# Splitting the first load of A on SyncE's queue into 32 and 96 partitions, in a batched 64x64 matmul

## The chip, the cores and the metric

The kernel runs on one core of a Trainium2 chip. The metric is the device time of one execution in microseconds (us); lower is better. Times come as a median of several runs; one further execution was recorded by the hardware profiler, and its trace is what the times of single instructions are read from.

## The reference

```python
def setup_inputs():
    return {
        "a": np.random.randn(1024, 64, 64).astype(np.float32),
        "b": np.random.randn(1024, 64, 64).astype(np.float32),
    }

def reference(a, b):
    return np.matmul(a, b).astype(np.float32)
```

There are 1024 independent products of two 64x64 matrices. A and B are 16.8 MB each and the output is as large, so 33.55 MB are read from HBM and 16.78 MB are written.

## The kernel before, in words

The 1024 products are cut in 16 steps `t` of 64 products for B and the output, and in 8 pairs of steps `s` of 128 products for A. One quarter `h` of a pair's A holds the matrices `4g + h`, with `g` from 0 to 31; each matrix is laid on four partitions, so a quarter is a tile of 128 partitions, each with one contiguous row of 1024 fp32 (4 KB). In HBM a quarter is 32 blocks of 16 KB, one block for each `g`.

A is converted to bf16, its 64x64 matrices are transposed in pairs of bf16 seen as one fp32, either on TensorE (`transpose`, L136, with copies out of PSUM by ScalarE at L144) or on VectorE (`transpose_dve`, L119; for the pairs 1, 2 and 3), and `spread` (L149) copies them into a block-diagonal weight tile `at_bd`. `cast` (L172) converts a step of B to bf16. `multiply` (L190) runs 64 matmuls a step against the block-diagonal weights and moves the results from PSUM to `o_sb`, mostly on ScalarE (L209). A step's output is stored one step later by `store`.

Loads go out on three DMA queues, in the order in which the program issues them:

- SyncE's queue (in the profile SPq, and q1 in the table of DMA queues): two quarters of the first A, B for the even steps, and the raw fp32 quarter `a_raw` of the later pairs of A.
- ScalarE's queue (ACTq, q10): the other two quarters of the first A, and B for the odd steps.
- GpSimd's queue (POOLq, q0): the converting loads of A to bf16 (`cast_load_a`, L70) and nearly all stores.

The order of the instructions is written out by hand under `tc.manual_schedule()`; tile pools and their semaphores decide only what waits. A load's completion is counted on a semaphore, and eight of these are shared in turn by the loads of SyncE's and ScalarE's queues; a load that takes a semaphore again waits for the load that had it.

The change is in `load_first_a` (L84). It borrows two output buffers `o_sb` for the four fp32 quarters `h` = 0 to 3 of pair 0, and issues quarters 0 and 2 on SyncE's queue and 1 and 3 on ScalarE's (L94). They are the first instructions on both queues. `regroup(0)` (L103) then converts the quarters into `a_bf` (L109), 0 and 2 on VectorE and 1 and 3 on ScalarE. On VectorE that comes after the clearing of `at_bd` (L250), and GpSimd clears the other block-diagonal tile in the same time (L252, L255). After the four conversions come 16 transposes of TensorE (L141), `spread(0)`, the cast of the first B on ScalarE, and the first `multiply`. The step loop (L262) runs the spread and the cast of step `t + 1` ahead of the multiply of `t`, and issues the B load of step `t + 3`.

Of the kernel before, what the change touches and what calls it, by code (L numbers as in the profile page):

```python
# [13 lines left out]
def kernel(  # L14
# [14 lines left out]
    nc = tc.nc  # L29
# [11 lines left out]
    a_v = a.rearrange("(s g h) (mp v) k -> s h g mp (v k)", h=4, g=32, v=16)  # L41
# [42 lines left out]
    def load_first_a():  # L84

        raw = [
            o_pool.tile([128, 8, 2, 2, 64], fp32, name="o_sb")[:].rearrange(
                "p gh j wl n -> p (gh j wl n)"
            )
            for _ in range(2)  # L90
        ]
        parts = [raw[h % 2][:, 1024 * (h // 2) : 1024 * (h // 2) + 1024] for h in range(4)]
        for h in range(4):
            (nc.scalar if h % 2 else nc.sync).dma_start(out=parts[h], in_=a_v[0, h])  # L94
        a_tiles[0] = parts

    def load_b(t):
# [144 lines left out]
    with tc.manual_schedule():  # L242
        first_cast = cast_load_a(1)
        load_first_a()

        nc.vector.memset(warm[:, 0:1], 0.0)
# [76 lines left out]
```

## Time and profile before

| | before |
|---|---|
| median of 3 runs | 133.37 us (133.36 to 133.55) |
| the profiled execution | 133.69 us |
| its span, first to last instruction | 131.8 us |
| VectorE (DVE) busy | 102.0 us, 77% |
| ScalarE (ACT) busy | 88.1 us, 67% |
| TensorE (PE) matmuls busy | 60.3 us, 46% |
| GpSimd (POOL) busy | 33.2 us, 25% |
| DMA queues q0, q1, q10, share of 16 engines | 52.7%, 28.5%, 20.2% |
| HBM traffic over the span | 382 GB/s |

The span is cut in 40 slices of 3.3 us in the page of the profile, and each digit of a row there is the busy share in tenths. A DMA share can be over 1, as the packets of one DMA engine overlap a little. In the tables of instructions, SPq and ACTq are the sequencers that issue DMAs; the time of such an issue is not the time of the transfer. A wait is put down to the instruction or the DMA that ended it. The profiled execution is 0.32 us longer than the median of the runs, and 1.89 us of its time lie outside its span.

### The profile page before, as it was taken

How to read it: one execution, taken by the hardware profiler on the slowest of the kernel's cores; microseconds unless marked ns; L12 is line 12 of the kernel's file. 1: busy time of each engine (PE TensorE's matmuls, PEld its weight loads, DVE VectorE, ACT ScalarE, POOL GpSimd, SP SyncE). 2: the span in 40 equal slices, each digit the busy share in tenths (PEclk: the TensorE clock that was granted, in tenths of full speed). 3: DMA queues.
4: the chain of work that ended last, by engine and by line, in shares of the span. 5: the costliest groups of instructions: out<-in, count | busy, mean ns of one | idle time of the engine just before them, and what ended most of it. 6: DMA issues, size and time to landing. Idle time of an engine off the chain costs nothing.

```text
span 131.8 us, 2749 instructions
## 1 busy us (share of the span) xinstructions
PE 60.3 (46%) x1104; PEld 57.2 (43%) x1104; DVE 102.0 (77%) x144; ACT 88.1 (67%) x158; POOL 33.2 (25%) x45
## 2 busy tenths in 40 slices
PE   0003701964090270908971983199369615366000
PEld 0003501964090270908961963198368614355000
DVE  5932099807999996999999999599999997798300
ACT  2123605599949069492999989559969998339930
POOL 6991000042016300618120204300420212041200
PEclk9999999999999998555599599559968999679755
DMA  3999999999999999999999999999999999999993
GB/s 71 344 341 306 306 306 297 270 313 319 328 316 401 347 310 308 399 390 395 314 288 364 400 397 359 306 303 389 393 390 392 395 391 393 391 405 402 402 379 135
DMA packets 18252, 44.99 MB, mean 341 GB/s; under 512 B 1088, under 2 KB 2112, under 8 KB 18240
## 3 DMA queue, kind: packets, MB, share of 16 engines
q0 software_dynamic: 7120, 21.24, 52.7%
q1 hardware_dynamic: 6064, 13.63, 28.5%
q10 hardware_dynamic: 5056, 9.96, 20.2%
q8 instruction: 8, 0.13, 0.4%
q14 instruction: 4, 0.03, 0.1%
HBM read 33.55 MB, written 16.78 MB: 382 GB/s over the span
## 4 chain that ended last, share of the span: by engine, by line
DMA 53%; ACT 16%; DVE 14%; PE 6%; issue 5%; SPq 2%; DVEq 0%; ACTq 0%
DMA b_sb<-in_b_dram 53%; ACT o_sb L209 13%; PE o_ps L221 5%; DVE at_bd L167 4%; DVE b_bf L176 4%; DVE at_bd L157 2%; ACT b_bf L176 1%; DVE at_sb L131 1%; DVE o_sb L209 1%; DVE a_bf L112 1%; SPq L94 1%; ACT a_bf L129 1%; SPq L100 1%; ACT b_bf L183 1%; DVE a_bf L115 0%
## 5 line engine op out<-in xcount | busy, mean ns | idle before, releaser
L209 ACT COPY o_sb<-o_ps 64x512 f32<-64x512 f32 x112 | 65.0, 581 | 18.5 <-PE o_ps L221 14.3
L221 PEld LDWEIGHTS <-at_bd 128*128 128x128 bf16 x1024 | 45.3, 117 | 51.5 <-DVE b_bf L176 39.6
L221 PE MATMUL o_ps<-b_bf,at_bd 128*128 128x64 bf16 x960 | 45.7, 223 | 47.1 <-DVE b_bf L176 36.8
L167 DVE COPY at_bd<-at_sb 32x1024 f32<-32x1024 f32 x40 | 29.5, 737 | 5.9 <-ACT at_sb L144 4.9
L198 POOL DMA_DIRECT2D out_dram<-o_sb x16 | 17.1, 1068 | 53.8 <-ACT at_sb L144 21.1
L157 DVE COPY at_bd<-at_sb 32x512 f32<-32x512 f32 x48 | 21.6, 451 | 1.1
L73 POOL DMA_DIRECT2D a_sb<-in_a_dram x21 | 12.0, 588 | 37.2 <-DVE at_sb L131 34.0
L176 DVE CAST b_bf<-b_sb 128x2048 bf16<-128x2048 f32 x14 | 17.4, 1245 | 4.3 <-DMA b_sb<-in_b_dram 4.0
L141 PE MATMUL at_ps<-identity,a_bf 128*128 128x128 f32 x80 | 13.3, 336 | 11.9 <-ACT a_bf L109 11.9
L141 PEld LDWEIGHTS at_ps<-identity,a_bf 128*128 128x128 f32 x80 | 12.2, 181 | 11.9 <-issue 11.9
L144 ACT COPY at_sb<-at_ps 128x512 f32<-128x512 f32 x20 | 10.8, 591 | 2.4 <-PE at_ps L141 2.0
L131 DVE STREAM_TRANSPOSE at_sb<-a_sb 128x512 f32<-128x512 f32 x9 | 8.7, 1055 | 0.0
L131 DVE STREAM_TRANSPOSE at_sb<-a_bf 128x512 f32<-128x512 f32 x3 | 3.1, 1044 | 4.6 <-ACT a_bf L129 4.6
L109 ACT CAST a_bf<-o_sb 128x1024 bf16<-128x1024 f32 x2 | 2.1, 1045 | 5.9 <-DMA o_sb<-in_a_dram 5.9
L209 DVE COPY o_sb<-o_ps 64x512 f32<-64x512 f32 x8 | 5.5, 689 | 0.2
L109 DVE CAST a_bf<-o_sb 128x1024 bf16<-128x1024 f32 x2 | 3.2, 1599 | 2.9 <-DMA o_sb<-in_a_dram 2.9
L176 ACT CAST b_bf<-b_sb 128x2048 bf16<-128x2048 f32 x1 | 1.9, 1899 | 4.5 <-DMA b_sb<-in_b_dram 4.5
L112 DVE COPY a_bf<-a_sb 128x3072 bf16<-128x3072 bf16 x4 | 4.2, 1046 | 0.0
L183 ACT CAST b_bf<-b_sb 128x512 bf16<-128x512 f32 x2 | 1.1, 614 | 4.5 <-DMA b_sb<-in_b_dram 4.5
L250 DVE MEMSET at_bd<- 128x4096 f32 x1 | 3.5, 3472 | 0.8 <-issue 0.8
L209 DVE COPY o_sb<-at_ps 64x256 f32<-64x256 f32 x8 | 3.4, 422 | 0.5 <-PE at_ps L221 0.4
L129 ACT CAST a_bf<-a_raw 128x1024 bf16<-128x1024 f32 x3 | 3.1, 1045 | 0.1
(16 smaller groups left out, 15.4 us busy)
## 6 DMA issues: line engine op xcount, KB each, us to landing
out_dram<-o_sb POOLq DMA_DIRECT2D x14, 1024.0 KB, 21.5
a_sb<-in_a_dram POOLq DMA_DIRECT2D x21, 256.0 KB, 14.2
a_raw<-in_a_dram SPq DMA_DIRECT2D x7, 512.0 KB, 17.5
o_sb<-in_a_dram SPq DMA_DIRECT2D x2, 512.0 KB, 6.8
o_sb<-in_a_dram ACTq DMA_DIRECT2D x2, 512.0 KB, 7.5
out_dram<-o_sb POOLq DMA_DIRECT2D x2, 512.0 KB, 5.9
out_dram<-o_sb SPq DMA_DIRECT2D x2, 256.0 KB, 4.6
out_dram<-o_sb ACTq DMA_DIRECT2D x2, 256.0 KB, 4.6
```

What stands on the lines that cost most here:

```text
L73: nc.gpsimd.dma_start(out=a_sb[:, h, :, :].rearrange("p v k -> p (v k)"), in_=a_v[s, h], single_packet=True)
L109: copy(a_bf[:, :, h, :], a_sb[h].rearrange("p (v k) -> p v k", v=16))
L112: nc.vector.tensor_copy(a_bf[:, :, 0:3, :], cast_sb[:].rearrange("p h v k -> p v h k"))
L131: nc.vector.transpose(at_tiles[s][:, h].rearrange("p g w mp vo -> p w vo g mp"), pairs.rearrange("p (vo w kp) -> p w vo kp", vo=4, w=4),)
L141: nc.tensor.transpose(at_ps[:, vo, :], a_cols[:, 4 * vo + 2 * j + wl, :], identity[:])
L144: nc.scalar.copy(at_tiles[s][:, :, 2 * j + wl, :, :], at_ps[:].rearrange("p vo (g mp) -> p g mp vo", mp=4),)
L157: nc.vector.tensor_copy(bd[rows, 8 * i : 8 * i + 8, :, h, :, :].rearrange("p g w mp vo -> p (g w) (mp vo)"), at_sb[block : block + 32, h]. ...
L167: nc.vector.tensor_copy(bd[rows, :, :, h, :, :].rearrange("p g w mp vo -> p (g w) (mp vo)"), at_sb[rows, half].rearrange("p g w mp vo -> p ...
L176: (nc.vector.tensor_copy if t else nc.scalar.copy)(b_bf[:], b_sb[:])
L198: store_queue(t, lo).dma_start(out=o_v[t, :, lo : lo + n, :], in_=o_sb[:, lo : lo + n].rearrange("p gh j wl n -> p (gh j wl n)"),)
L209: copies[2 * par + wl](dst, src)
L221: nc.tensor.matmul(o_ps[:, gl, g % 2, j, :], at_bd[:, j, g, :, u], b_bf[:, g, 64 * u : 64 * u + 64], start=(u == 0), stop=(u == 1),)
```

## The change

The load of quarter 0 is issued as two loads on the same queue: blocks `g` = 0 to 7, which are partitions 0 to 31, and then blocks `g` = 8 to 31, which are partitions 32 to 127. The bytes, the rows of 4 KB and the destination are the same. Quarters 1, 2 and 3 are loaded as before. VectorE's conversion of quarter 0 is not split, so it needs both parts. On SyncE there is one DMA instruction more; the instructions of the other engines and their order are unchanged. As one load more takes a semaphore, the later loads of SyncE's and ScalarE's queues each take the next one in turn.

```diff
         for h in range(4):
-            (nc.scalar if h % 2 else nc.sync).dma_start(out=parts[h], in_=a_v[0, h])
+            queue = nc.scalar if h % 2 else nc.sync
+            for lo, hi in ((0, 8), (8, 32)) if h == 0 else ((0, 32),):
+                queue.dma_start(out=parts[h][4 * lo : 4 * hi], in_=a_v[0, h, lo:hi])
         a_tiles[0] = parts
```

The lines of the kernel after this place are numbered two higher in the kernel after.

## The prediction

> **What bounds the kernel now.** I read the page's slices first, then the DMA queues, then the timeline of the first 24 us, then the DMA packets of its first stage, VectorE's waits and the chain that ended last.
>
> ```profile
> DVE  5932099807999996999999999599999997798300
> DMA  3999999999999999999999999999999999999993
> q0 software_dynamic: 7120, 21.24, 52.7%
> q1 hardware_dynamic: 6064, 13.63, 28.5%
> q10 hardware_dynamic: 5056, 9.96, 20.2%
> ```
>
> The DMA engines are full from the second slice to the last but one; the queues' shares add up to 101% of 16 engines. VectorE is nearly full from slice 10 to 35. So a transfer is late because of what is queued ahead of it, and more work on the DMA engines can't be made up by an earlier issue.
>
> ```profile
> 0.74 1.28 SPq L94 DMA_DIRECT2D o_sb<-in_a_dram  x2
> 1.69 3.47 DVE L250 MEMSET at_bd<- 128x4096 f32 x1 [0.83 <-issue]
> 2.49 0.73 SPq L100 DMA_DIRECT2D b_sb<-in_b_dram  x1
> 3.27 7.69 SPq L81 DMA_DIRECT2D a_raw<-in_a_dram  x1
> 5.17 2.50 DVE L109 CAST a_bf<-o_sb 128x1024 bf16<-128x1024 f32 x1
> 6.46 1.05 ACT L109 CAST a_bf<-o_sb 128x1024 bf16<-128x1024 f32 x1 [2.65 <-DMA o_sb<-in_a_dram]
> 10.58 0.69 DVE L109 CAST a_bf<-o_sb 128x1024 bf16<-128x1024 f32 x1 [2.90 <-DMA o_sb<-in_a_dram]
> 10.76 1.04 ACT L109 CAST a_bf<-o_sb 128x1024 bf16<-128x1024 f32 x1 [3.25 <-DMA o_sb<-in_a_dram]
> 11.42 0.71 SPq L100 DMA_DIRECT2D b_sb<-in_b_dram  x1
> 11.90 3.65 PE L141 MATMUL at_ps<-identity,a_bf 128*128 128x128 f32 x16 [11.90 <-ACT a_bf L109]
> 20.71 1.90 ACT L176 CAST b_bf<-b_sb 128x2048 bf16<-128x2048 f32 x1 [4.54 <-DMA b_sb<-in_b_dram]
> ```
>
> The columns are start, duration, instruction and, in brackets, the idle time before it and what ended it. The conversion of quarter 0 (5.17) has no DMA wait: it starts when the memset is done at 5.16. The trace has the quarter landing at 5.14. VectorE then sits idle for 2.90 us until quarter 2 is there. So quarter 0 itself is not on the path; quarters 2 and 3 (landing at 10.55 and 10.74) are, since TensorE's transposes wait for the last conversion. The first B load, third on SyncE's queue, is next: ScalarE waits 4.54 us for it.
>
> ```profile
> DVE b_bf L176 <- DMA b_sb<-in_b_dram: 4.0, 3, 1.6
> 102.61 14.88 DMA b_sb<-in_b_dram
> ```
>
> The first line is the only large wait of VectorE after 36 us; the second, from the chain in order of time, is the last B load, which brings ScalarE to the final step at 117.5. The path keeps coming back to a transfer, and it is the last of a transfer's 16 completions that counts: of the B load behind the wait of 1.6 us, fifteen came by 82.37 and the sixteenth at 83.71; of the last B load, fourteen by 116.07 and the others at 117.01 and 117.49. One or two DMA engines run behind the rest.
>
> **The issue.** One DMA issue more on SyncE. L94's two take 1.28 us together, 0.64 each with the pause between them; this bounds a 32-partition issue from above, the 0.38 us of the small final stores from below. Behind it on SyncE: the rest of quarter 0, quarter 2, the first B, the first `a_raw`. Each is issued 0.4 to 0.64 us later. For quarter 2 and B that is hidden, since their predecessors on the queue are still moving; for `a_raw` too, whose issue already stands 7.69 us because the queue is full. Counted at nothing. Without that cover it would be the whole 0.64.
>
> **The semaphores.** The counters move on by one, so the third B load (11.42), which had waited for none, now waits for the first part. That is there by about 5, and SyncE is held in the `a_raw` issue until 10.96: nothing. The `a_raw` loads after it wait for quarter 1 (landed 6.44) and for the second part instead of quarters 0 and 1, and ScalarE's first in-loop B load for quarter 3 instead of 2: all landed long before. Without SyncE's hold, the third B load alone would wait, for some 2 us.
>
> **The conversion.** It needs both parts. If the second lands 0.64 late, it starts at 5.8 instead of 5.17 and ends at 8.3, before quarter 2. The 2.90 us of idle time hide it; they cover a delay of up to 2.9 us.
>
> **The DMA engines.** This is the term that counts. A full quarter has 32 blocks in HBM and can be dealt evenly to 16 engines: 8 rows of 4 KB each. The parts have 8 and 24 blocks. The trace shows no load of this shape, so I bound it: dealt row by row the parts put 8 rows on each engine as before, at a cost of 0; dealt in whole blocks from the first engine on, 8 blocks reach 8 engines with 4 rows each, and 24 blocks divide evenly over 12 at most, 8 rows each. Then eight engines carry 12 rows, four carry 8 and four none. A row's price is in the first stage:
>
> ```profile
> DMA packets 338, 1.16 MB, mean 291 GB/s; under 512 B 31, under 2 KB 31, under 8 KB 338
> q1 hardware_dynamic: 149, 0.54, 48.9%
> q10 hardware_dynamic: 143, 0.52, 35.5%
> ```
>
> This is the window from 2 to 6 us, 64 engine-us. q10's 35.5% are 22.7 us; 0.52 MB are 127 rows; 0.18 us a row. q1's, with the cold start in it, are 0.24. I take 0.18, from the warmer queue, because the added rows come after the first. Four more rows are 0.72 us on eight engines (0.96 by q1's price). As these engines have no pause to give it back in, it stays in every later transfer that has its last completion there, up to the end. The upper bound is the queue order: with three queues in turn, each of the four rows lets one packet of each of the others pass. A row and a packet of each other queue at some 0.18 us, the small B packets at half, are 0.45 us, so four turns make 1.8 us for quarter 2 and the first B. Below nothing is possible too, by the four relieved engines, below. I take 0.72: the load on the path goes by total work, not by turns, once later queues are full; the turns' 1.8 is a high end for the start only, and VectorE's 4.0 us of waits can take some of it in.
>
> The Trainium skill ("DMA: Bandwidth & Descriptors", "Why a DMA increments its semaphore by 16 and not by 1") says that a DMA from SyncE uses the largest number of engines up to 16 that divides the outermost sizes of both its sides, the lowest-numbered ones: 8 and 12 here. By it the whole-block case is the one that happens, and the sum is the same 0.72; no run here shows it yet. The same page's "Rules for kernel authors" says that a transfer split into disjoint partition parts gains nothing, as the parts share the engines. By that rule alone the term would be 0, or the 0.64 of an issue.
>
> **The sum.** 0 + 0 + 0 + 0.72 us against the profiled 133.69 us: 134.41. The profiled execution stands 0.32 above the median, so I expect 134.1 as a median (133.37 + 0.72).
>
> **The rivals.** First, no change. The rows are dealt evenly, or the engines that bound the end are the four that keep 8 rows. For it: all loads of the trace make 16 completions, and the only load touched is off the path by 2.9 us. Against it: nothing in an 8-block load makes an even deal natural. Time: 133.4, within 0.2% (0.27 us), about what a measurement of this kernel can tell.
>
> Second, faster, by one mechanism: the DMA engines that run behind lie among the four relieved ones. These lose 8 rows, 1.44 us. The waits at 83.71 and 117.49 end with one and two late completions; if the late ones move up by 1.44, the next engine decides, 1.34 earlier in the first place (82.37) and 1.42 in the second (116.07) less the 0.72 that this one may have gained: 0.6 to 0.7 net. Time: 132.7. It decides only when both late engines of the second place are among the four; one alone leaves 117.01 or later. Against it: the last stores, whose completions form an early group of seven (129.20 to 129.92) and a late one of nine (130.31 to 130.77), so that at least one of the late nine is among the eight with more rows.
>
> Third, the turns of the queue count in full: quarter 2 lands at 12.3, the first B at 22.5, ScalarE's cast and all that follows it start 1.8 us later, and VectorE, 90% busy and more from there on, doesn't give it back. Time: 135.2. Against it: VectorE waits for B three times later on, and a full DMA queue does not care when it was filled.
>
> **How the numbers follow.** The forecast, 133.7 to 134.6, has 0.5; the third rival 0.11 (134.6 to 135.2); no change 0.16; faster 0.23. Slower by over 0.2% is then 0.61. The range has to leave out no more than 2 in 10: from 132.8, most of the faster case, to 135.1, most of the turns. The likeliest case's own range is 133.7 to 134.6.
>
> **What would show it.** Right: three issues of quarter loads on SyncE; the second part landing at 5.5 to 6; VectorE's first conversion starting with the DMA as its releaser; quarters 2 and 3 landing at 11.2 to 12 and the first transposes at 12.5 or later; the first B at 21.4 or later; the DMA slices as full as before, and the last stores 0.7 later. Wrong: quarter loads landing when they did (the even deal), or the start later and the end not (VectorE's waits took it in), or completions of the late B loads closing up (the relief). A start as forecast with an end that moved for another cause would refute the step in which the load is carried to the end.

## The result, and the profile after

The kernel after takes 135.82 us as a median of 4 runs (135.65 to 135.94), the one before 133.39: 2.43 us slower, a ratio of 1.0179 with a 95% interval of 1.0164 to 1.0195. The way was forecast, the size was not: 134.1 with a range up to 135.1. The profiled execution took 135.78 us, its span is 134.0. One run of all those below (141.74 us, the split 8 + 8 + 16 of the later quarters) was slow, 1.5% longer than the fastest of its kernel, and is left out.

The page's slices and queues of the kernel after, as they were shown of before:

```profile
DVE  5502208990899999899999999499999999598700
...
DMA  3999999999999999999999999999999999999994
...
q0 software_dynamic: 7120, 21.24, 52.1%
q1 hardware_dynamic: 6068, 13.63, 28.4%
q10 hardware_dynamic: 5056, 9.96, 21.0%
```

The bytes are the same and the DMA engines are as full (the three queues add up to 101.5% of 16 engines). VectorE stands at 0, 2, 2 and 0 tenths in slices 3 to 6, where it had 3, 2, 0 and 9: its first spreads come a slice later. The timeline of the start, kernel after (columns as in the prediction):

```profile
0.74 2.51 SPq L96 DMA_DIRECT2D o_sb<-in_a_dram  x3
...
4.52 11.17 SPq L81 DMA_DIRECT2D a_raw<-in_a_dram  x1
4.89 1.04 ACT L111 CAST a_bf<-o_sb 128x1024 bf16<-128x1024 f32 x1 [1.35 <-DMA o_sb<-in_a_dram]
...
10.96 1.04 ACT L111 CAST a_bf<-o_sb 128x1024 bf16<-128x1024 f32 x1 [5.02 <-DMA o_sb<-in_a_dram]
12.56 0.69 DVE L111 CAST a_bf<-o_sb 128x1024 bf16<-128x1024 f32 x1 [7.39 <-DMA o_sb<-in_a_dram]
15.52 0.69 DVE L111 CAST a_bf<-o_sb 128x1024 bf16<-128x1024 f32 x1 [2.27 <-DMA o_sb<-in_a_dram]
16.36 3.65 PE L143 MATMUL at_ps<-identity,a_bf 128*128 128x128 f32 x16 [16.36 <-DVE a_bf L111]
...
24.38 1.90 ACT L178 CAST b_bf<-b_sb 128x2048 bf16<-128x2048 f32 x1 [3.75 <-DMA b_sb<-in_b_dram]
```

VectorE now waits 7.39 us for the second part of quarter 0, which lands at 12.46 (the whole quarter landed at 5.14). That is not what holds the start up: the conversion that now comes last and releases TensorE's transposes is that of quarter 2, which lands at 15.50 instead of 10.55, behind the second part on its queue. The transposes start 4.5 us later, the first B lands 3.7 us later (24.36). ScalarE's and GpSimd's first loads gained: quarter 1 landed at 4.87 instead of 6.44. The first packet on SyncE's queue started at 3.85 us instead of 2.19, behind ScalarE's at 2.17.

The first part shows 8 completions of transfers (4.88 to 5.32), the second 12 (11.31 to 12.46); the rest of the sixteen is added at once at the start (2.09 and 2.92). This is the deal that the Trainium skill's rule gave ("DMA: Bandwidth & Descriptors", "Why a DMA increments its semaphore by 16 and not by 1"), and here trace and rule agree.

What the queues did from 8 to 12 us, first before, then after:

```profile
DMA packets 573, 1.29 MB, mean 322 GB/s; under 512 B 61, under 2 KB 61, under 8 KB 573
...
q0 software_dynamic: 192, 0.33, 44.2%
q1 hardware_dynamic: 189, 0.46, 32.2%
q10 hardware_dynamic: 192, 0.49, 31.1%
```

```profile
DMA packets 385, 0.96 MB, mean 241 GB/s; under 512 B 47, under 2 KB 47, under 8 KB 385
...
q1 hardware_dynamic: 127, 0.46, 44.6%
q0 software_dynamic: 129, 0.23, 31.0%
q10 hardware_dynamic: 129, 0.27, 30.8%
```

The engines are full in both, but a packet takes longer: on SyncE's queue 44.6% of 64 engine-us over 127 packets are 0.22 us, where it had been 0.11 (partly small B packets then); 4 KB rows alone took 0.18 to 0.32 us there instead of 0.17. ScalarE's packets went from 0.10 to 0.15 us, though fewer of them were large; GpSimd's stayed at 0.15, its 4-byte packets included.

To compare executions I count **work done**: every packet at what its kind usually takes in the kernel before (4 KB rows 0.171 us on SyncE's queue and 0.160 on ScalarE's, 2 KB packets 0.095 and 0.084 as in the first 20 us, 1 KB 0.047, GpSimd's loads 0.172 and stores 0.168), summed and divided by 16. It is an estimate, good to about 0.1 us. The kernel after is 0.1 us of such work behind before at 6 us, 1.4 at 12 us and still at 30 us, and 2.2 to 2.3 from 36 to 120 us; the two spans differ by 2.2 us. So two places lose the time: 6 to 12 us, and 30 to 36 us. In both it is lost by slower packets and not by idle DMA engines: counted as the packets really took, the DMA engines were busy for the same time up to 13.4 us within 0.1 us, and within 0.2 up to 50 us. The second place, from 30 to 34 us, before and after:

```profile
q1 hardware_dynamic: 169, 0.60, 40.9%
q0 software_dynamic: 166, 0.31, 40.9%
q10 hardware_dynamic: 170, 0.35, 23.6%
```

```profile
q1 hardware_dynamic: 253, 0.76, 60.0%
q10 hardware_dynamic: 270, 0.55, 44.8%
```

After, GpSimd's queue (q0) has nothing to move from 29.1 to 34.8 us; before, that pause lasted 0.4 us. Its next loads wait for a buffer that VectorE's transposes of pair 1 free, and these are late. The waits, before and after:

```profile
POOL a_sb L73 <- DVE at_sb L131: 34.0, 3, 15.6
```

```profile
POOL a_sb L73 <- DVE at_sb L133: 38.1, 3, 20.2
```

The longest of the three waits is 4.6 us longer. The other two queues fill the engines and move as many bytes (1.31 MB after, 1.28 before), but with slower packets: 4 KB rows at 0.19 to 0.21 us, B's 2 KB at up to 0.12. Why they are slower without GpSimd's beside them is not shown. ScalarE's queue is empty for a while too (20.9 to 29.4 us after, 20.2 to 27.1 before), and nothing is lost there.

### The profile page after: what moved, and what is told of

Same layout as the page of the kernel before. It is cut to its first block, busy times and chain, and to the rows that moved or that the text cites. A ratio compares the mean times of both kernels' runs of the same rounds, so it can differ in the third digit from the quotient of the medians.

```text
span 134.0 us, 2751 instructions
## 1 busy us (share of the span) xinstructions
PE 61.8 (46%) x1104; PEld 58.8 (44%) x1104; DVE 100.3 (75%) x144; ACT 88.1 (66%) x158; POOL 33.0 (25%) x45
## 3 DMA queue, kind: packets, MB, share of 16 engines
q1 hardware_dynamic: 6068, 13.63, 28.4%
## 4 chain that ended last, share of the span: by engine, by line
DMA 39%; DVE 23%; ACT 18%; PE 7%; issue 6%; SPq 2%; ACTq 1%; DVEq 0%
DMA b_sb<-in_b_dram 39%; ACT o_sb L211 15%; DVE at_bd L159 8%; PE o_ps L223 7%; DVE b_bf L178 5%; DVE at_bd L169 4%; DVE at_sb L133 4%; SPq L96 2%; ACT b_bf L178 1%; ACT a_bf L131 1%; DVE o_sb L211 1%; DVE a_bf L114 1%; ACTq L102 1%; ACT b_bf L185 1%; DVE a_bf L117 0%
## 5 line engine op out<-in xcount | busy, mean ns | idle before, releaser
L223 PEld LDWEIGHTS <-at_bd 128*128 128x128 bf16 x1024 | 46.5, 119 | 48.8 <-DVE b_bf L178 37.1
L223 PE MATMUL o_ps<-b_bf,at_bd 128*128 128x64 bf16 x960 | 47.0, 226 | 44.6 <-DVE b_bf L178 35.3
L169 DVE COPY at_bd<-at_sb 32x1024 f32<-32x1024 f32 x40 | 29.4, 735 | 5.4 <-ACT at_sb L146 4.4
L111 DVE CAST a_bf<-o_sb 128x1024 bf16<-128x1024 f32 x2 | 1.4, 694 | 9.7 <-DMA o_sb<-in_a_dram 9.7
```

The lines of the kernel that those rows point to most:

```text
L169: nc.vector.tensor_copy(bd[rows, :, :, h, :, :].rearrange("p g w mp vo -> p (g w) (mp vo)"), at_sb[rows, half].rearrange("p g w mp vo -> p ...
L223: nc.tensor.matmul(o_ps[:, gl, g % 2, j, :], at_bd[:, j, g, :, u], b_bf[:, g, 64 * u : 64 * u + 64], start=(u == 0), stop=(u == 1),)
```

## The experiments

Each kernel was timed in rounds against the kernel before on the same chip, except one that was executed once more, which is named. In the text, "later" and "slower" are against before. The table at the end of this section has the profiled executions in one view.

**Even parts.** 64 and 64 partitions instead of 32 and 96.

```diff
-            for lo, hi in ((0, 8), (8, 32)) if h == 0 else ((0, 32),):
+            for lo, hi in ((0, 16), (16, 32)) if h == 0 else ((0, 32),):
```

> Quarter 0 split as 64 + 64 partitions (16 + 16 blocks), still two loads on SyncE's queue. Theory U (uneven deal: 8 and 12 engines instead of 16 put 12 rows on eight engines and slow the rows): with 16 blocks each part is dealt to 16 engines, so the loss is gone: 133.2 to 133.8 us. Theory L (lost lead: one more issue on SyncE ahead of the bulk of quarter 0 lets ScalarE's and GpSimd's loads go first, and SyncE's later loads are served in turns behind them): the loss stays, 135 us or more, with quarter 2 landing after 14 us and the first B after 23 us.

134.66 us, 1.0068 [1.0046, 1.0090]. Between the two theories: 1.4 of the 2.4 us go with the uneven deal, 1.0 us stays. Sixteen completions for each part; quarter 2 lands at 12.66, the first B at 22.46.

**Even deal with the same sizes.** 32 and 96 partitions, but from consecutive rows in HBM (`a_rows`, a view of A by rows). The data are others, so the products of the first quarter are not those of the reference.

```diff
-                queue.dma_start(out=parts[h][4 * lo : 4 * hi], in_=a_v[0, h, lo:hi])
+                rows = a_v[0, h, lo:hi] if h else a_rows[0, 4 * lo : 4 * hi]
+                queue.dma_start(out=parts[h][4 * lo : 4 * hi], in_=rows)
```

> The split 32 + 96 of the kernel after, but quarter 0 is read from 128 consecutive rows of A instead of its own blocks (other data: the first quarter's products are of the wrong matrices). The HBM side's outermost size is then 32 and 96, both multiples of 16, so both parts are dealt to 16 engines, two and six rows each. Theory U: 133.2 to 133.8 us, sixteen completions for each part. Theory L: as the kernel after, 135.5 us or more, since the number of issues and their sizes are the same. If only the shift of the rows against the partitions slows them (96 rows over 16 engines do not sit as 128 do), rows of 0.25 us and more are seen here too.

134.02 us, 1.0024 [1.0013, 1.0036]. Sixteen completions for each part. So two loads of 32 and 96 partitions cost only 0.4 us here; the rest of the 2.4 goes with the blocks. That is more than the deal over engines: the rows lie side by side in HBM, the three issues took 1.54 us together instead of 2.51, and SyncE's first packet came at 1.76, ahead of ScalarE's (2.18), so this kernel does not separate slow rows from the lost lead. On SyncE's queue rows of 0.21 to 0.26 us are seen only from 5 to 6 us.

**The same split on quarter 2.**

```diff
-            for lo, hi in ((0, 8), (8, 32)) if h == 0 else ((0, 32),):
+            for lo, hi in ((0, 8), (8, 32)) if h == 2 else ((0, 32),):
```

> The same split in 8 and 24 blocks, but of quarter 2, the second load on SyncE's queue; quarter 0 is whole and leads. Theory U: the same uneven rows, in the same queue, so the same loss: 135.4 to 136 us. Theory L: SyncE's queue keeps its lead of 8 rows, so most of the loss is gone: 133.4 to 134.2 us, first B landing at 20.7 to 21.5 us.

135.32 us, 1.0120 [1.0099, 1.0141]. SyncE leads again (first packet 2.17, quarter 0 whole at 4.84), and two thirds of the loss stay. The lost lead seems the smaller part. Rows on both hardware queues are slow from 8.5 to 12 us, when the 96-partition part moves.

**A small load first.**

```diff
+        nc.sync.dma_start(out=small[:], in_=a_rows[0, 0:128, 0:16])
         for h in range(4):
```

> The kernel before, with one small load (128 rows of 64 bytes, into a tile that nothing reads) ahead of quarter 0 on SyncE's queue; all loads are dealt to 16 engines. Theory U: no uneven rows, so 133.3 to 133.8 us. Theory L: quarter 0 is issued one issue later (0.64 us), ScalarE's quarter 1 goes first, and the loss is as in the kernel after: 135 us or more.

(`small` is a tile that nothing reads.) 134.68 us, 1.0075 [1.0055, 1.0094], with no uneven deal at all: between the two theories. Its executions differ, from 133.72 to 135.09, and the profiled one was the fastest. It was executed and profiled once more, on another chip:

> The kernel with the small load ahead of quarter 0, profiled once more. If its usual 134.7 us comes from a late start of the arithmetic (theory F), the first multiply is at 23.7 us or later and GpSimd's queue runs empty near 30 us; if it comes from DMA-engine work lost in the first microseconds, the first multiply is near 22.9 and the work done by 13.4 us is 0.7 us or more behind.

134.47 us beside 133.38 of before on that chip, one execution each. Quarter 0 lands at 7.40 in the first profile, at 8.29 in the second, where GpSimd's first load went ahead of it (first packet 3.79 instead of 5.00). The first multiply is at 22.86 and 23.43; only the second execution is clearly behind at 50 us, by 0.6 us (the first by 0.1). The multiply came a little sooner than the 23.7 expected for late arithmetic, and GpSimd's queue moved 103 packets from 30 to 34 us instead of 166, so it was not empty all that time (its pause went from 28.4 to 31.6 us); but only 0.1 us were lost by 13.4 us. This speaks for the second place of loss rather than for work lost at the start. The pause began earlier, as GpSimd's first loads did, and ended later, as the arithmetic was later.

**Three parts without a load on 12 engines.**

```diff
-            for lo, hi in ((0, 8), (8, 32)) if h == 0 else ((0, 32),):
+            for lo, hi in ((0, 8), (8, 16), (16, 32)) if h == 0 else ((0, 32),):
```

> Quarter 0 in three loads of 8, 8 and 16 blocks (32, 32 and 64 partitions). Dealt to 8, 8 and 16 engines, so eight engines carry 12 rows and eight carry 4: as uneven as in the kernel after, or more, but without a load on 12 engines. Theory C (the count of rows on the fullest engines is what costs): 135.3 us or more. Theory R (the 12-engine load of 96 partitions makes rows slow, 0.25 to 0.32 us each, also those of ScalarE's queue beside it): rows stay under 0.22 us and the time is near the kernel with 64 + 64, 134.3 to 135.0.

135.10 us, 1.0105 [1.0087, 1.0122], between theory R (up to 135.0) and theory C (from 135.3). From 8 to 12 us:

```profile
q0 software_dynamic: 171, 0.32, 41.6%
q1 hardware_dynamic: 170, 0.60, 40.6%
q10 hardware_dynamic: 167, 0.36, 25.5%
```

The packets are nearly back (0.15 us on q1 with 0.60 MB, mostly 4 KB rows), and the work lost by 13.4 us falls from 1.4 to 0.5. But quarter 2 still lands at 14.73, behind twelve rows of quarter 0 on eight engines, the first multiply is 3.1 us late, and another 0.7 us of work are lost by 50 us. Slow rows and late arithmetic are thus two things.

**The split turned round.**

```diff
-            for lo, hi in ((0, 8), (8, 32)) if h == 0 else ((0, 32),):
+            for lo, hi in ((0, 24), (24, 32)) if h == 0 else ((0, 32),):
```

> The split turned round: 24 blocks (96 partitions) first, 8 blocks second. The count of rows on each engine is that of the kernel after. Theory C: 135.5 to 136. Theory R: the slow rows come with the 96-partition load wherever it is, but at the head of the queue it moves largely before the others start, so less is slowed: 134.3 to 135.2. Theory L (the lost lead alone): the first part now has 96 rows, so most of the loss is gone, 133.5 to 134.3.

135.75 us, 1.0153 [1.0133, 1.0172]. The time is in the band of theory C, above that of theory R: at the head of the queue the 96-partition part slows rows too (0.24 to 0.29 us from 4.5 to 6.5). ScalarE still went first.

**ScalarE's loads after its table load**, in the kernel after and, as a control, in the one before.

```diff
-        load_first_a()
-
         nc.vector.memset(warm[:, 0:1], 0.0)
         nc.scalar.copy(warm[:, 1:2], warm[:, 0:1])
+        load_first_a()
```

> The kernel after, but ScalarE loads its activation table and makes its first small copy before it issues its quarters 1 and 3, so SyncE's first part goes first. Theory L: the lead is SyncE's again, so the first B lands at 21.5 or sooner and the time is within 0.5 us of the kernel before with the same order on ScalarE. Theories C and R: the 96-partition load is still there, so 1.3 us or more is lost against that kernel.

> Control for the kernel with ScalarE's loads after its table load: the kernel before with the same order on ScalarE. SyncE leads as before; quarters 1 and 3 are issued some 1.6 us later, still before their turn: 133.2 to 134.0 us by all theories.

136.04 us, 1.0172 [1.0148, 1.0196]; control 133.71, 1.0001 [0.9987, 1.0014]. So 2.3 us are lost against the control, as theories C and R had it. The first kernel does not test the lead: ScalarE's issue came only 0.17 us later, at 0.91, and its packets still went first (2.34, SyncE's 4.61). Even an issue begun 0.17 us sooner does not give the 8-block load the lead; in the control the whole quarter had it.

**Late arithmetic alone.** No load is changed; ScalarE repeats conversions.

```diff
+    def again(a_bf, a_sb):
+        for h in (1, 3, 1, 3):
+            nc.scalar.copy(a_bf[:, :, h, :], a_sb[h].rearrange("p (v k) -> p v k", v=16))
...
+            again(a_bf, a_sb)
...
+        first = a_tiles[0]
...
+        again(abf_tiles[0], first)
         cast(0)
```

> The kernel before with nothing changed in its loads; ScalarE repeats four conversions of quarters 1 and 3 (1.04 us each, the same data once more) after the first ones, and four more ahead of the cast of the first B, so that the first multiply starts at 26.3 us or a little later, as in the kernel after, instead of 22.7. Theory F (late compute feeds back: GpSimd's loads for the next pair wait for VectorE, their queue runs empty near 30 us, and the DMA engines lose work there): 0.6 to 1.1 us slower than before, 134.1 to 134.6. If late compute is absorbed by the full DMA queues: within 0.3 us of before. If the start is on the path in full: 3.5 us slower.

134.42 us, 1.0052 [1.0034, 1.0070], as theory F had it. The first multiply is at 25.46, 2.8 us late (less than planned), and that costs 0.8 us. Nothing is lost by 13.4 us (0.1 us), 0.7 us by 50 us, and from 30 to 34 us the picture is that of the kernel after, with no q0:

```profile
q10 hardware_dynamic: 341, 0.70, 53.4%
q1 hardware_dynamic: 196, 0.67, 49.5%
```

**The later raw quarters split**, all seven, quarter 0 whole; three deals. The first is shown; the others have (0, 16), (16, 32) and (0, 8), (8, 16), (16, 32).

```diff
-        nc.sync.dma_start(out=a_raw[:].rearrange("p v k -> p (v k)"), in_=a_v[s, 3])
+        flat = a_raw[:].rearrange("p v k -> p (v k)")
+        for lo, hi in ((0, 8), (8, 32)):
+            nc.sync.dma_start(out=flat[4 * lo : 4 * hi], in_=a_v[s, 3, lo:hi])
```

> The kernel before, with quarter 0 whole, but each of the seven later raw quarters of A split in 8 and 24 blocks. Theory R (the 12-engine load makes rows slow, some 1.2 us of DMA work each): 138 to 142 us, with rows of 0.25 us and more around each of these loads. Theory C (only the count, four more rows of 0.17 us on eight engines, 0.7 us each): 137 to 138.5 us, rows of 0.17 us. If a split in the middle of full queues costs nothing: 133.4 to 134.

> Control: the seven raw quarters of A split in 16 and 16 blocks, each part on 16 engines with four rows each. Theories R and C: 133.3 to 134.5 us. If one more load on the queue costs by itself, as the lost lead did at the start: 135 us or more.

> The seven raw quarters of A split in 8, 8 and 16 blocks: 8, 8 and 16 engines, twelve rows on eight engines as with 8 and 24, four on the other eight, but no load on 12 engines. Theory R: most of the loss of the 8 and 24 split is gone, 133.5 to 135.5 us, rows under 0.2 us. Theory C: the same as the 8 and 24 split, 137 us or more.

8 + 24: 140.38 us, 1.0496 [1.0451, 1.0542]. 16 + 16: 135.89, 1.0153 [1.0124, 1.0182]. 8 + 8 + 16: 139.58 as the median of three runs, 1.0447 [1.0401, 1.0493]. Here theory R fails. 4 KB rows on SyncE's queue take 0.168 us as a mean after 20 us with 8 + 24, so the 12-engine load is not slow wherever it stands, and 8 + 8 + 16 loses nearly as much. Against the even split, the uneven deals cost (6.74 - 2.25) / 7 = 0.64 and (5.94 - 2.25) / 7 = 0.53 us a load, near the 0.72 that the prediction gave to the count; and the DMA share falls, to 0.77 from 120 to 130 us with 8 + 24 (0.99 before). Here the DMA engines are less full as well: the packets' own time, summed and divided by 16, grows by 2.9 us (134.2 to 137.1) with 8 + 24, the span by 6.4. The even split was no free control: in it, ScalarE's 2 KB packets took up to 0.15 us from 33 to 39 us, and its packets' own time grows by 2.0 us, as much as its span (1.9).

**Splits by columns.** Both parts keep all 128 partitions: quarter 0 as 256 + 768 columns, and, in another kernel, the seven raw quarters as 512 + 512.

```diff
-            (nc.scalar if h % 2 else nc.sync).dma_start(out=parts[h], in_=a_v[0, h])
+            queue = nc.scalar if h % 2 else nc.sync
+            for lo, hi in ((0, 256), (256, 1024)) if h == 0 else ((0, 1024),):
+                queue.dma_start(out=parts[h][:, lo:hi], in_=a_v[0, h][:, :, lo:hi])
```

> Quarter 0 split by columns, 256 and 768 of 1024, so that both loads have all 128 partitions and 32 blocks, and both go over 16 engines with 8 shorter rows each; one issue more on SyncE, as in the kernel after. Theory D (the loss comes from dealing partitions to other engines than a whole load): no slow rows, 133.3 to 134.2 us. Theory I (an issue more at the head of SyncE's queue costs by itself): 134.8 us or more.

> Quarter 0 whole; the seven later raw quarters of A split by columns, 512 and 512, both parts with all 128 partitions, 16 engines, 8 rows of 2 KB each. To be held against the split in 16 and 16 blocks, which also has 16 engines but 64 partitions in each part and took 2 us more than before. Theory D: 133.4 to 134.2 us, and ScalarE's 2 KB packets at 0.09 us all through. Theory I: as with 16 and 16 blocks, 135.5 us or more.

Quarter 0: 134.62 us, 1.0070 [1.0046, 1.0095], between the two theories. No slow rows after 5 us, hardly anything lost by 13.4 us (0.1), SyncE leads (2.19), and still 1.0 us slower: the first part holds only a quarter of the bytes, the other 768 columns come behind ScalarE's first load and beside GpSimd's (landing 9.16), quarter 2 at 12.53, the first multiply 1.3 us late, 0.7 us of work lost by 50 us. The raw quarters: 137.63 us, 1.0301 [1.0274, 1.0328]. Theory D is wrong for these: with all 128 partitions in both parts they lose more than 16 + 16. Their 2 KB packets take 0.09 us as a mean over the kernel, but not throughout: ScalarE's took 0.11 from 60 to 65 us. The packets' own time grows by 2.5 us (134.2 to 136.7), the span by 3.6; the rest is DMA engines less full near the end (a share of 0.84 from 120 to 130 us, 0.99 before). Halved packets in a queue that is served in turns could add to that; this was not tested.

**Quarter 0 in four loads of 8 blocks.**

```diff
-            for lo, hi in ((0, 8), (8, 32)) if h == 0 else ((0, 32),):
+            for lo, hi in ((0, 8), (8, 16), (16, 24), (24, 32)) if h == 0 else ((0, 32),):
```

> Quarter 0 in four loads of 8 blocks, all dealt to the same eight engines: sixteen rows on each of these, none on the others. Theory C (count): worse than the kernel after, 136.5 us or more. Theory D, in the form that rows are slow where an engine writes partitions that another engine writes in a whole load: the first two parts (partitions 0 to 63) at 0.17 us a row, the third and fourth (64 to 127) slow, and ScalarE's rows beside them slow; 135 to 136.5 us.

136.42 us, 1.0206 [1.0187, 1.0224], 0.1 us below theory C's band and at the upper end of theory D's. The rows of the first two parts take 0.17 us. From 10 to 11.5 us, while the third part moves and eight of quarter 2's sixteen completions come (11.35 to 11.58), rows take 0.19 to 0.24, and 2 KB packets on ScalarE's queue up to 0.14. While the fourth part moves (landing 13.23) SyncE's rows are at 0.17 again, and only the 2 KB packets stay slow (0.10 to 0.14 until 13 us), so theory D holds in part. First multiply 4.4 us late.

**Earlier arithmetic.** GpSimd's first three loads come later.

```diff
-        first_cast = cast_load_a(1)
         load_first_a()
...
-        load_a(1, first_cast)
+        load_a(1)
```

> The kernel before, with GpSimd's first three converting loads (of pair 1, needed at 23 us) issued after its clearing of the weight tile, some 4 us later, so that the quarters of pair 0 and the first B have the DMA engines for themselves at first: quarters 2 and 3 at 8 to 9 us instead of 10.6, first multiply 1 to 2 us earlier. If the start of the arithmetic is on the path: 132 to 132.8. If the sum of the DMA engines' work sets the end: 133.2 to 133.8, no change.

133.82 us, 1.0016 [1.0004, 1.0028]. The first multiply is 1.0 us earlier, and nothing is gained.

| profiled execution | first multiply, us later | work behind at 13.4 us | pause of GpSimd's queue near 30 us | work behind at 50 us | medians: us slower |
|---|---|---|---|---|---|
| kernel before | 0 | 0 | 0.4 | 0 | 0 |
| kernel after | 3.66 | 1.4 | 5.7 | 2.2 | 2.43 |
| 96 + 32 | 2.42 | 1.4 | 2.6 | 1.7 | 2.14 |
| quarter 2 split | 1.87 | 1.0 | 2.8 | 1.3 | 1.68 |
| 4 loads of 8 blocks | 4.38 | 0.8 | 6.5 | 2.0 | 2.79 |
| 8 + 8 + 16 blocks | 3.12 | 0.5 | 5.7 | 1.2 | 1.49 |
| 64 + 64 | 1.77 | 0.6 | 3.4 | 1.0 | 1.02 |
| columns 256 + 768 (3 KB rows at 0.13 us) | 1.33 | 0.1 | 4.5 | 0.7 | 0.99 |
| late arithmetic | 2.80 | 0.1 | 5.0 | 0.7 | 0.78 |
| small load first, second profile | 0.77 | 0.1 | 3.2 | 0.6 | 1.09 (single executions) |
| consecutive rows | 0.51 | 0.3 | 1.0 | 0.3 | 0.38 |
| GpSimd's loads later | -0.98 | 0.1 | none | 0.0 | 0.19 |

The work behind at 50 us gives the time lost to within 0.8 us. What the kernel after lost is 1.4 us by slow packets up to 12 us, and 0.8 us while GpSimd's queue is empty behind late arithmetic. The second loss goes with the length of that pause better than with the first multiply: 0.3 us for pauses of 2.6 and 2.8 us, 0.6 to 0.8 us for 4.5 to 5.7, 1.2 us for 6.5.

## Why the prediction was right or wrong

**The way** was right, and in part with the term that the forecast named: with an even deal 1.4 of the 2.4 us are gone, though not by the mechanism of the forecast (below). The other 1.0 had been counted at nothing.

**The bound** held: the DMA engines are full, and work that they lose is lost at the end, about one for one (2.2 us of each in the profiled executions). Earlier arithmetic without more work done gained nothing.

**The issue**, counted at nothing, was wrong. SyncE's first issues on the chain that ended last, before and then after:

```profile
0.74 0.65 SPq L94
1.44 0.58 SPq L94
```

```profile
0.74 0.87 SPq L96
1.67 0.84 SPq L96
2.55 0.70 SPq L96
```

The three issues took 0.87, 0.84 and 0.70 us, longer than the bound of 0.64, and the cover that I named, "their predecessors on the queue are still moving", was not there at the head: SyncE's 96 rows came behind quarter 1 and beside GpSimd's first load. The column split, which has one load more but neither an uneven deal nor slow rows, costs 1.0 us.

**The semaphores** held: the third B load is issued at 16.14, after the `a_raw` issue that ends at 15.69; no new wait shows.

**The conversion** failed with the issue: "if the second lands 0.64 late" became 7.3 us (12.46 for 5.14), beyond the 2.9 us of cover. It still did not set the start: quarter 2, 5.0 us late itself, was converted after it and released the transposes.

**The DMA engines**: the deal was right, 8 and 12 engines, and in the middle of the kernel the uneven deal costs 0.53 to 0.64 us a load, close to the 0.72. At the head the first step that failed is the price of a row in this term: 0.18 us from the warm queue, while rows measured 0.22 to 0.32 from 7.5 to 11.5 us, those of ScalarE's queue beside them too. By 13.4 us that is 1.4 us instead of 0.72. It is not four added rows at the usual price: the slowed packets of all engines add up to it, and the engines' busy time is unchanged. Why they are slow is not settled. It goes with parts that hold only some of the partitions (0.5 us without the 12-engine load, 0.1 with the column split), but not always: 8 + 24 of the later quarters moves at 0.168 us a row.

**The third rival** had the mechanism that I left at 0.11. Quarter 2 landed even later than its 12.3 (15.50), the first B later than its 22.5 (24.36). The argument against it, that "a full DMA queue does not care when it was filled", is the second step that failed: the DMA engines stayed full, but GpSimd's queue ran dry for 5.7 us, since its loads wait for VectorE, and the packets of the other two were slower in that time. Late arithmetic alone, 2.8 us late, costs 0.78 us. So a late start costs neither the forecast's nothing nor, as this rival had it, all of the delay, but about a quarter of it there; the pause of the queue tells more than the delay.

**The faster rival** did not happen: the four engines with fewer rows did run ahead in the kernel after (quarter 2 complete on four at 12.38 to 12.75, on twelve at 14.48 to 15.50; the first B at 21.86 to 22.22 and 23.64 to 24.36), and both of these loads still ended with the other twelve.

The Trainium skill advises against two transfers to disjoint halves of the partitions, since both share the same engines ("DMA: Bandwidth & Descriptors", "Rules for kernel authors"). The runs agree that nothing is gained, and show a loss of 1.0 us for the even split and 2.4 for this one.

## What to carry to other kernels

Before splitting a load, look at the outermost size on both sides of each part: parts that the DMA engines can't share evenly leave the load at the pace of the fullest engines (0.53 to 0.64 us a load here in the middle of the kernel). At the head of a queue that competes with others, a part that comes second falls behind the first loads of all other queues, so splitting a load that must be complete before it is used delays it. And when transfers bound a kernel, ask which queue waits for a buffer that late arithmetic will free: here the delay came back there, as slower packets on the other queues.

## What the runs showed of the hardware that was not expected

- The issue of an 8-block load took 0.87 us against 0.65 for the whole quarter, and its first packet came at 3.85 us instead of 2.19: a quarter of the bytes started later.
- Rows on SyncE's and ScalarE's queues can slow together, from 0.17 and 0.16 us to 0.32 and 0.29, while GpSimd's loads keep 0.17 to 0.18 a packet.
- With GpSimd's queue empty, full DMA engines moved 4 KB rows at 0.19 to 0.21 us instead of 0.17; how long that queue was empty goes with the work lost (0.3 us for 2.6 us, 1.2 us for 6.5).
- Two executions of one kernel (the small load first), on two chips, served the first loads in another order; one took 0.1 us longer than before, the other 1.1.
- Seven loads split by columns, with 2 KB packets instead of 4 KB, cost 4.0 us in full queues, though these packets took 0.09 us as a mean.
